# A two-layer diffusion step on one Trainium2 core: low parts of a weight corner, copies of products, convolution taps, one tile's scaling and one pair of transposes issued in another sequence

## The chip, the cores and the metric

The kernel runs on one core of one Trainium2 chip. The metric is the time of one execution on the device in microseconds (us). Of before there are three timed runs and one profiled run.

## What is computed

One inference step of a trunk of two layers, on 512 latent tokens and 128 prompt tokens of width 1024. Layer 0 mixes tokens by neighbourhood attention on a 2-D grid, layer 1 by grouped-query attention. After each mixer stands a gated ConvFFN of width 2816, each sub-layer between two RMS norms, with shift, scale and gate from a conditioning vector (adaLN). Cut to the part in which most of the change lies:

```python
def conv_ffn(h, w_up, conv_w, conv_b, w_down):
    u = h @ w_up
    up = jnp.pad(u, ((0, 0), (1, 1), (0, 0)))
    u = up[:, :-2] * conv_w[0] + up[:, 1:-1] * conv_w[1] + up[:, 2:] * conv_w[2] + conv_b
    a, gt = jnp.split(u, 2, axis=-1)
    return (jax.nn.silu(a) * gt) @ w_down
```

All is float32; the outputs are the two token streams and the new keys and values of both layers.

## The kernel before, in words

**Two parts for each operand.** Each float32 weight or activation is cast on ScalarE to a high part (`wh`, `vh`, `ah`, `B`, `hF`'s parts) and the rest goes into a low part (`wl`, `vl`, `al`), a `tensor_sub` on VectorE or GpSimd. A product is three passes: high x high, low x high, high x low. `wsplit` (L170) does this for a weight on its way in, `split` (L1291) inside the ffn.

**The up-projection.** In `ffn` the hidden width is cut into 22 pieces of 128, p = 0 to 21, each with a value half (i = 0) and a gate half (i = 1). The 640 tokens are two halves of `TH` = 320. For p = 0 and 1 (`PLAIN` = 2) `plain0` and `plain1` multiply the weight's halves plainly. From p = 2 on, the 2 x 2 blocks of weight and activation are multiplied with seven products in the place of eight (a Winograd form): `product(m, p)` is product m, twelve matmuls of 128x320. `of_m` says which weight block each takes: product 6 and 3 the sum `(0, p)`, product 7 and 5 the sum `(1, p)`, product 1 and 2 the value block `w`, product 4 the corner `a`. The weights' sums are formed by `block_sums` (four `wr` instructions on VectorE, L1314 to L1317, in place in the raw weights, so that the fourth can only follow the corner's `al`, which reads them); `sum_parts` casts them to `wh` (ScalarE) and `wl` (GpSimd from p = 3 on); `value` and `corner` make `vh`/`vl` and `ah`/`al`.

**The order of products.** For each p the loop at L1488 runs m = 6, 5, 1 of p+1, 7, 2 of p+1, 3, 4. `evict` takes each out of PSUM: `copied` (ScalarE copies `c1`, `u2`, `v5`), sums into the convolution's input `C` on VectorE (L1400, L1409, L1413), and a copy for product 4 (L1417). After product 3, `conv_value` runs the width-3 convolution of the value half: `t` on ScalarE (L1378), two taps on VectorE (L1381, listed in `taken`), then SiLU, `sl`. After product 4, `conv_gate` does the same for the gate half and multiplies (`act`, L1392, `marks[4]`); `store` sends it to DRAM. In layer 0 a group of 24 adaLN matmuls (`ada`) stands between some of the products.

**The down-projection.** `load_dn` (L1248) brings a weight and an activation piece `ain` back, casts it (`ahi`) and forms its low part `alo` on VectorE (L1261; the list `lows`). The accumulators are `acc`. At the end of a layer `Finish` makes the residual, the norm and the next sub-layer's input: `shifted` (L416) scales a token tile in two halves, `turns` transposes it.

**What sets the order.** TensorE's instructions are chained one behind the other (`pe`, L111), so that their order is the order of the program text. For the other engines a scheduler sets the order, from data and buffers; `behind(a, b)` (L125) adds that `a` comes after `b`. Each engine then runs its list strictly in that order, each instruction waiting for its data and for the release of the buffer that it writes.

**The attention's end.** In layer 0 the query and key projections run as a stream of small steps (`stream`, L1115) between the heads. Each head pair ends with `tail`, which transposes the prompt's new keys (`tk`, for the output). Behind the stream, `early` begins the output projection, `m0.part0(t, p)`, tile `y`.

Of the kernel before, what the change touches and what calls it, by code (L numbers as in the profile page):

```python
# [105 lines left out]
def hybrid_step(ctx: ExitStack, tc: tile.TileContext, A, O):  # L106
# [57 lines left out]
    def x_in(t):  # L164
        return A["x_sample"][0, t * P : (t + 1) * P, :] if t < 4 else A["x_prompt"][0]

    queue = []


    def wsplit(src, a, b, low=None, own=None, pin=False, after=None, high=None, low_after=None):  # L170
        q = own or wp
        raw = wp.tile([P, a, b], F32, tag="wr", name="wr")
        i = nc.sync.dma_start(raw, src)
        if queue:
            behind(i, queue.pop())
        hi = q.tile([P, a, b], F32R, tag="wh", name="wh")
        i = nc.scalar.copy(hi, raw)  # L177
        lo = q.tile([P, a, b], F32R, tag="wl", name="wl")
        j = (low or nc.vector).tensor_sub(lo, raw, f32(hi))  # L179
        if high:  # L180
            behind(i, high[0])
        if after:
            behind(i, after[0])
            behind(j, after[1])
        if low_after and not low:
            behind(j, low_after)
        if pin:
            tc.keep_in_program_order(i)
            tc.keep_in_program_order(j)
        return hi, lo  # L190
# [148 lines left out]
    class Finish:  # L339
# [75 lines left out]

        def shifted(self, t):  # L416
            xm, r = self.xm[t]
            return [
                nc.vector.scalar_tensor_tensor(
                    xm[:, c], xm[:, c], r, self.sh[:, c], op0=ALU.mult, op1=ALU.add  # L420
                )
                for c in HALF
            ][0]

        def last(self, copied, added, low):

# [420 lines left out]
    with l_na:  # L847
# [253 lines left out]
            nc.vector.tensor_sub(lo, of0[p], f32(hi))  # L1101


        items, marks = [], {}

        def put_qk(p):
            it, tail = na_qk_items(p)
# [10 lines left out]
        def stream():  # L1118
            items[0][0]()
            tail = None  # L1120
            for n, (load, parts) in enumerate(items):
                for i, part in enumerate(parts):
                    part()
                    if n + 1 == len(items) and i in OW:
                        m0.weights(0, OW[i], nc.gpsimd)
                    if i == 1 and n + 1 < len(items):
                        items[n + 1][0]()
                    if i == 4 and tail:
                        tail()
                        tail = None  # L1130
                    yield
                tail = marks.get(n + 1, tail)
            if tail:
                tail()

        work = stream()
        l_ada = ExitStack()
# [14 lines left out]
        for h in range(H):  # L1152
            nxt = Head(h + 1) if h + 1 < H else None
            g = h // 4
            pr = h % 4 == 1
            order = (ORDER if h < 13 else ORDER2)[h % 2] if h else ORDER0
            for i, step in enumerate(order):
                if step == "f":
                    if i < len(order) - 1 or h % 4 or not h:
                        fill()  # L1160
                elif step == "a":
                    next(ada0, None)
                elif step[0] == "s" and nxt:
                    nxt.scores(int(step[1]))
                elif step[0] == "t":
                    head.turns(int(step[1]))
                elif step == "v":
                    values((before, head))
                if pr and step == "p0":
                    sides = []  # L1170
                    for hh in range(4 * g, 4 * g + 4):
                        qs, kh, kl = qk_of[hh // 2]
                        b = hh % 2
                        sides.append((qs[b][:, QW - P :], kh[b][:, T:], kl[b][:, T:]))
                    pp = prompt_scores(ap, sides)
                if pr and step == "p1":
                    pth = prompt_turn(ap, pp, "pk", NPK)
                if pr and step == "p2":
                    po = bk.get("po")
                    for j in range(2):  # L1180
                        for b in range(2):
                            mm(po[64 * b : 64 * b + 64, j * P : j * P + P], vts_of[g][:, 4, 2 * j + b, :],
                               pth[:, 2 * j + b, :], start=True, stop=True)
                    for j in range(2):
                        nc.scalar.copy(of0[2 * g + j][:, NS:T], po[:, j * P : j * P + P])
                    bk.put(po)
            before = head
            head = nxt
            if h == 11:
                def early(ps, *rows_):  # L1190
                    for ts in rows_:
                        for p in ps:
                            for t in ts:
                                m0.part0(t, p)
                                yield

                work = chain(work, early(range(OEARLY), range(2)))
                drain(ada0)
                l_ada.close()
                epool = l_na.enter_context(pool("o0e", 1))  # L1200
                osp0.extend([epool.tile([P, T], F32R, name=f"o{i}{p}") for i in "hl"] for p in range(OEARLY))
                for p in range(OEARLY):
                    o_split(p)
            if h == 12:
                drain(work)
                r_h0.close()
                hpool = r_na.enter_context(pool("o0h", 1, "right"))
                osp0.extend([hpool.tile([P, T], F32R, name=f"o{i}{p}") for i in "hl"] for p in range(OEARLY, KC))
                for p in range(OEARLY, 4):
                    o_split(p)  # L1210
                m0.weights(0, 3)
                for p in range(4, 6):
                    o_split(p)

                work = chain(early(range(OEARLY, 6), range(2)), early(range(6), range(2, NT)))
            if h == 13:
                o_split(6)
# [21 lines left out]
    def ffn(l, hT, hT_close, xold, xnew, nxt, todo, late, late_close, side, back, first, fin0, after=None):  # L1239
# [33 lines left out]
        with ExitStack() as s2:  # L1273
# [15 lines left out]
                return [own.tile([P, n, P], F32R, tag=x, name=x) for x in tags]  # L1289

            def split(src, hl, low):  # L1291
                nc.scalar.copy(hl[0], src)  # L1292
                return low.tensor_sub(hl[1], src, f32(hl[0]))  # L1293

            def plain(p, i, low):
# [9 lines left out]

            def corner(p):
                ws["a", p] = pair_of(sw2, ("ah", "al"), 4)
                split(raws[p, 1][:, 4:8, :], ws["a", p], nc.vector)

            def block_sums(p):  # L1310

# [10 lines left out]
                done.add((p, i))  # L1322
                fetch()

            banks, cs, ts, small, outs, taken, marks, held = {}, {}, {}, {}, deque(), [], {}, []

            def block_product(u, w, h, b, first, last=True, lows=False):

# [67 lines left out]
            def evict(m, p, u):  # L1396
# [5 lines left out]
                elif m == 6:  # L1402
                    copied("u2", p, u)
                elif m == 5:
                    copied("v5", p, u)
                elif m == 7:
                    v = small.pop(("v5", p))
                    for c, dst in pieces(p, 1):
                        marks[7] = nc.vector.tensor_add(dst, u[:, c], v[:, c])  # L1409
                elif m == 3:  # L1410
                    v = small.pop(("u2", p))
                    for c, dst in pieces(p, 0):
                        marks[3] = nc.vector.tensor_add(dst, u[:, c], v[:, c])  # L1413
                    bk.put(banks.pop(("z", p)))
                    conv_value(p)
                else:
                    nc.scalar.copy(block(p, 1, 0), u)  # L1417
                    bk.put(banks.pop(("x", p)))
                    conv_gate(p)
# [52 lines left out]
            for n, c in enumerate(chunks):  # L1472
                plain1(*c)
                if n == 1:
                    corner(PLAIN)
                    block_sums(PLAIN)
                    sum_parts(0, PLAIN, nc.vector)
                    sum_parts(1, PLAIN, nc.vector)
                    drain(more)
            value(PLAIN + 1, nc.gpsimd)  # L1480
            corner(PLAIN + 1)
            bk.drop(4)
            psy.close()
            ct = s2.enter_context(pool("ct", space=PSUM))
# [12 lines left out]
            for p in range(PLAIN, FC):  # L1497
                nx = p + 1 if p + 1 < FC else None
                for m, q in ((6, p), (5, p), (1, nx), (7, p), (2, nx), (3, p), (4, p)):
# [7 lines left out]
                            lds.append(load_dn(len(lds), *HB[0], after=taken[-3]))  # L1507
                    elif m == 7:
                        store()
                        if nx:  # L1510
                            sum_parts(0, nx, nc.gpsimd)
                        else:
                            behind(lows[0], marks[7])
                            if ada and not nxt:
# [6 lines left out]
                    elif m == 3:  # L1521
                        if not nx:
                            lds.append(load_dn(len(lds), *HB[0], low=False))
                            behind(lows[1], marks[3])
                            behind(taken[-2], lows[1])
                        elif nx + 1 < FC:
                            corner(nx + 1)
                    if ada:
# [17 lines left out]
        for grp, (c0, c1) in (((0, 1, 2), HB[0]), ((3, 4), HB[1])):  # L1546
# [8 lines left out]
            for k in range(FC - tail):  # L1555
                if len(lds) <= k:
                    lds.append(load_dn(k, c0, c1, after=taken[-3] if k == 2 and c0 == 0 else None))
                for t in grp:
                    if t != 2 or k >= DLEAD:
                        go(t, k, *lds[k])  # L1560
# [10 lines left out]
            for t in grp:  # L1571
# [7 lines left out]
                for i in range(tail):  # L1579
# [4 lines left out]
                        lds.append(load_dn(len(lds), *HB[1]))  # L1584
                    if t == 4 and after:
                        after(i)
                late.append(fin.end(t, acc[t][0], acc[t][1], fin.stat(acc[t][0])))
        fin.close()
        s.close()
# [502 lines left out]
```

## Time and profile before

| what | value |
|---|---|
| median of three timed runs | 1532.52 us (1531.22 to 1532.67) |
| profiled run, its own time | 1531.28 us |
| span of the profiled run | 1529.5 us |
| mean granted TensorE clock | 0.998 |
| TensorE (PE) busy | 1506.5 us, 98% of the span |
| VectorE (DVE) busy | 1029.7 us, 67% |
| ScalarE (ACT) busy | 853.6 us, 56% |
| GpSimd (POOL) busy | 701.1 us, 46% |

The span runs from the first to the last instruction; the run's own time holds 1.8 us more around it. PE is the matmul engine, PEld its weight load. In a timeline a row gives the start in us, how long it lasted, engine, line, operation, what was written and read with its shape, and in brackets how long the engine had been idle before and what released it. In the list of waits a row gives the engine and tile that waited, what for, the us in total, how often, and the longest.

### The profile page before, as it was taken

Reading aid. Unit: us, or ns where it says so; the run is one execution under the profiler, and the core shown is the slowest. Engines: PE = TensorE matmul, PEld = TensorE weight load, DVE = VectorE, ACT = ScalarE, POOL = GpSimd, SP = SyncE. Lnnn points to the kernel's source line nnn. Section 1 sums busy time; section 2 is a strip of 40 time slices with the busy share of each in tenths; the row PEclk is TensorE's granted clock in tenths of the full one; section 3 lists DMA queues with packets and bytes.
Section 4 is the critical chain, followed back from the end, with each engine's and each line's share of the span. In section 5 each row is a group of like instructions: output and inputs, shape, how many; then the busy total and the mean of one; then the engine's idle time right before and its main releaser. Section 6 shows DMA issues by size and latency. Waiting matters only on the chain.

```text
span 1529.5 us, 26196 instructions
## 1 busy us (share of the span) xinstructions
PE 1506.5 (98%) x9710; PEld 1338.6 (88%) x9710; DVE 1029.7 (67%) x1733; ACT 853.6 (56%) x1636; POOL 701.1 (46%) x572
## 2 busy tenths in 40 slices
PE   7999999999999999999999999999999999999998
PEld 6989989789999999988887878778899999998886
DVE  5544443659877667865748878773988888886454
ACT  5665564646655555654545447763666665564343
POOL 1655554332355455534444454442235665553433
PEclk9999999999999999999999999999999999999999
DMA  9755444263575655388575421015433334458663
GB/s 351 186 137 150 121 132 115 64 206 111 183 231 182 226 189 160 123 283 272 189 221 161 124 75 38 2 41 189 157 114 118 112 120 150 133 162 280 216 224 131
DMA packets 196667, 243.99 MB, mean 160 GB/s; under 512 B 11485, under 2 KB 153021, under 8 KB 196541
## 3 DMA queue, kind: packets, MB, share of 16 engines
q1 hardware_dynamic: 186924, 235.85, 47.7%
q10 hardware_dynamic: 9616, 6.48, 2.4%
q8 instruction: 76, 1.25, 0.3%
q14 instruction: 51, 0.41, 0.1%
HBM read 214.38 MB, written 26.34 MB: 157 GB/s over the span
## 4 chain that ended last, share of the span: by engine, by line
PE 66%; DVE 7%; issue 1%; ACT 1%; POOL 1%; DMA 0%; DVEq 0%; POOLq 0%; ACTq 0%
PE acc L118 19%; PE ux L118 17%; PE uz L118 9%; PE gp L118 5%; PE uy L118 4%; PE y L118 3%; PE po L118 2%; PE s L118 2%; PE tp L121 2%; PE ada L118 2%; DVE B L248 1%; DVE wl L179 1%; DVE nmg L1813 1%; DVE t L1381 0%; DVE pk L1832 0%
## 5 line engine op out<-in xcount | busy, mean ns | idle before, releaser
L1293 POOL TENSOR_TENSOR wl<-wr,wh 128x1024 fp32r<-128x1024 f32 x76 | 181.5, 2411 | 222.1 <-ACT wh L1292 211.4
L179 POOL TENSOR_TENSOR wl<-wr,wh 128x1024 fp32r<-128x1024 f32 x70 | 172.1, 2461 | 233.6 <-ACT wh L177 219.0
L118 PE MATMUL ux<-B,wh 128*128 128x320 f32 x832 | 198.7, 311 | 0.9 <-ACT u L1348 0.8
L1381 DVE SCALAR_TENSOR_TENSOR t<-C,cw,t 128x642 f32<-128x642 f32 x176 | 156.0, 886 | 48.6 <-ACT t L1378 48.0
L118 PE MATMUL acc<-wh,ahi 128*128 128x512 f32 x440 | 172.1, 391 | 0.3 <-DVE act L1392 0.3
L118 PE MATMUL acc<-wh,alo 128*128 128x512 f32 x440 | 172.2, 391 | 0.0
L118 PE MATMUL acc<-wl,ahi 128*128 128x512 f32 x440 | 172.0, 391 | 0.0
L177 ACT CAST wh<-wr 128x1024 fp32r<-128x1024 f32 x138 | 143.3, 1048 | 41.6 <-DMA wr<-in_ffn_w_down 31.9
L118 PE MATMUL uz<-B,wh 128*128 128x320 f32 x640 | 154.6, 310 | 0.0
L118 PEld LDWEIGHTS ux<-B,wh 128*128 128x128 f32 x832 | 142.8, 188 | 4.1 <-ACT u L1348 1.3
L1261 DVE TENSOR_TENSOR alo<-ain,ahi 128x384 fp32r<-128x384 f32 (+1 forms) x88 | 80.2, 928 | 85.3 <-ACT ahi L1259 84.3
L118 PE MATMUL ux<-B,wl 128*128 128x320 f32 x416 | 128.8, 310 | 0.0
L118 PE MATMUL qk<-hT,wh 128*128 128x384 f32 (+1 forms) x512 | 122.4, 315 | 0.0
L118 PEld LDWEIGHTS uz<-B,wh 128*128 128x128 f32 x640 | 110.4, 188 | 2.9 <-issue 1.2
L1292 ACT CAST wh<-wr 128x1024 fp32r<-128x1024 f32 x84 | 85.0, 1048 | 48.2 <-DVE wr L1317 47.8
L1293 POOL TENSOR_TENSOR vl<-wr,vh 128x1024 fp32r<-128x1024 f32 x38 | 99.1, 2609 | 21.7 <-ACT vh L1292 21.6
L179 DVE TENSOR_TENSOR wl<-wr,wh 128x1024 fp32r<-128x1024 f32 x68 | 89.1, 1324 | 20.3 <-ACT wh L177 19.7
L1378 ACT ACTIVATE t<-C,cw 128x642 f32<-128x642 f32 x88 | 78.5, 892 | 42.1 <-DVE C L1413 33.5
L118 PE MATMUL uz<-B,wl 128*128 128x320 f32 x320 | 99.0, 309 | 0.0
L118 PEld LDWEIGHTS acc<-wh,ahi 128*128 128x128 f32 x440 | 82.6, 188 | 18.3 <-issue 0.7
L118 PEld LDWEIGHTS acc<-wl,ahi 128*128 128x128 f32 x440 | 82.6, 188 | 17.9
L118 PEld LDWEIGHTS acc<-wh,alo 128*128 128x128 f32 x440 | 82.6, 188 | 17.6
(263 smaller groups left out, 3858.8 us busy)
## 6 DMA issues: line engine op xcount, KB each, us to landing
wr<-in_ffn_w_up SPq DMA_DIRECT2D x88, 512.0 KB
wr<-in_ffn_w_down SPq DMA_DIRECT2D x88, 512.0 KB
wr<-in_ada_w SPq DMA_DIRECT2D x72, 512.0 KB
act<-act SPq DMA_DIRECT2D x44, 321.0 KB
wr<-in_na_w_qkv SPq DMA_DIRECT2D x24, 512.0 KB
mod<-modrow SPq DMA_DIRECT2D x20, 512.0 KB
ain<-act SPq DMA_DIRECT2D x44, 192.0 KB
wf<-in_ada_w SPq DMA_DIRECT2D x16, 512.0 KB
```

What stands on the lines that cost most here:

```text
L118: pe(nc.tensor.matmul(*a, **k))
L121: pe(nc.tensor.transpose(*a, **k))
L177: i = nc.scalar.copy(hi, raw)
L179: j = (low or nc.vector).tensor_sub(lo, raw, f32(hi))
L248: return nc.vector.tensor_sub(lo, src, f32(hi))
L1261: i = nc.vector.tensor_sub(lo[:, 0 : c1 - c0], ain[:, 0 : c1 - c0], f32(hi[:, 0 : c1 - c0]))
L1292: nc.scalar.copy(hl[0], src)
L1293: return low.tensor_sub(hl[1], src, f32(hl[0]))
L1378: nc.scalar.activation(t, taps(0), AF.Identity, bias=cw[:, 3, n : n + 1], scale=cw[:, 1, n : n + 1])
L1381: nc.vector.scalar_tensor_tensor(t, taps(d), cw[:, w, n : n + 1], t, op0=ALU.mult, op1=ALU.add))
L1813: self.red[i] = nc.vector.tensor_reduce(nm, sv, axis=AX.XY, op=ALU.min)
```

## The change

The arithmetic, the tiles and the number of matmuls stay as they are. Five places get another sequence.

1. The last head pair's `tail` (the transposes `tk`) is not issued at the end of the stream but by `early`, behind the first `m0.part0` of tile 1 (list `ends`).
2. At the ffn's start the low part `al` of the corner of p = 2 goes behind the fourth `plain0` sum (`summed[1]`).
3. The low part `al` of the corner of p = 3 goes behind the last sum of product 7 of p = 2 (`marks[7]`); the cast `wh` of the sum `(0, 3)` goes behind the copy `v5` of p = 2 (`marks[5]`).
4. Around the first loads of the down-projection the ties of `alo` change: the second goes behind the last tap, the fourth behind `act`, and a tap is no longer behind the second.
5. At the end of layer 0 the two halves of the scaling of token tile 3 go behind the low part `wl` of the weight loaded last.

The diff, cut to its core:

```diff
 def wsplit(...):
         j = (low or nc.vector).tensor_sub(lo, raw, f32(hi))
+        lowered[:] = [j]
...
 def stream():
-            if tail:
-                tail()
+            ends.append(tail)
...
                             for t in ts:
                                 m0.part0(t, p)
+                                if ends and t:
+                                    ends.pop()()
                                 yield
...
             def split(src, hl, low):
-                nc.scalar.copy(hl[0], src)
+                i = nc.scalar.copy(hl[0], src)
+                high[:] = [i]
                 return low.tensor_sub(hl[1], src, f32(hl[0]))
...
                 elif m == 5:
-                    copied("v5", p, u)
+                    marks[5] = copied("v5", p, u)
...
                 if n == 1:
-                    corner(PLAIN)
+                    behind(corner(PLAIN), summed[1])
                     block_sums(PLAIN)
...
             value(PLAIN + 1, nc.gpsimd)
-            corner(PLAIN + 1)
+            low = corner(PLAIN + 1)
...
                     elif m == 7:
                         store()
+                        if p == PLAIN:
+                            behind(low, marks[7])
                         if nx:
                             sum_parts(0, nx, nc.gpsimd)
+                            if p == PLAIN:
+                                behind(high[0], marks[5])
...
                             lds.append(load_dn(len(lds), *HB[0], low=False))
-                            behind(lows[1], marks[3])
-                            behind(taken[-2], lows[1])
+                            behind(lows[1], taken[-1])
...
                     lds.append(load_dn(k, c0, c1, after=taken[-3] if k == 2 and c0 == 0 else None))
+                    if k == 3 and c0 == 0:
+                        behind(lows[k], marks[4])
...
                     if t == 4 and after:
                         after(i)
+                        if i == tail - 1:
+                            for j in fin.moved:
+                                behind(j, lowered[0])
```

`corner` returns its low part, and `shifted` keeps its two instructions in `self.moved`. TensorE's order differs in the transposes `tk` alone. On the other engines the scheduler's order changes at more places than the ties name. The instructions below are listed by line, operation, tile with buffer number and shape; line numbers after the change are a few higher.

ScalarE in layer 0, around products 6 of p = 2 to 4 of p = 2, before. `wh_4928` and `wh_4948` are the casts of the two sums of p = 3, `ah_4997` that of the corner of p = 4, `vh_4954` that of its value block:

```order
L1292 CAST wh_4928<-wr_4435 128x1024
L1348 COPY u2_4868<-ux_4430 128x320
L1292 CAST wh_4948<-wr_4503 128x1024
...
L1292 CAST vh_4954<-wr_4739 128x1024
L1378 ACTIVATE t_4842<-C1_4582,cw0_82 128x2x321
L1387 ACTIVATE sl_4846<-t_4842 128x642
L1378 ACTIVATE t_4848<-C1_4582,cw0_82 128x2x321
L1292 CAST ah_4997<-wr_4745 128x512
```

ScalarE at the same place, after:

```order
L1295 CAST vh_4954<-wr_4739 128x1024
L1383 ACTIVATE t_4842<-C1_4582,cw0_82 128x2x321
L1392 ACTIVATE sl_4846<-t_4842 128x642
L1295 CAST ah_4997<-wr_4745 128x512
L1383 ACTIVATE t_4848<-C1_4582,cw0_82 128x2x321
L1295 CAST wh_4928<-wr_4435 128x1024
L1295 CAST wh_4948<-wr_4503 128x1024
```

The two casts `wh` have moved from around the copy `u2` of p = 2 to behind `ah_4997` and the next `t`. In layer 1 they stand likewise behind `ah`, the copy `C`, `sl` and `t`. On GpSimd the low part `vl` of p = 4 now stands ahead of the two `wl` of p = 3.

VectorE in layer 0, from the corner of p = 3 on, before (`al_4809` is its low part, the four `wr` are the sums, `t` the conv taps):

```order
L1293 TENSOR_TENSOR al_4809<-wr_4503,ah_4808 128x512
L1314 TENSOR_TENSOR wr_4503<-wr_4503 128x512
L1315 TENSOR_TENSOR wr_4503<-wr_4435,wr_4503 128x512
L1316 TENSOR_TENSOR wr_4435<-wr_4503,wr_4435 128x512
L1317 TENSOR_TENSOR wr_4435<-wr_4435 128x512
L1381 SCALAR_TENSOR_TENSOR t_4830<-C0_4465,cw0_82,t_4830 128x2x321 x2
L1381 SCALAR_TENSOR_TENSOR t_4836<-C0_4465,cw0_82,t_4836 128x2x321
L1409 TENSOR_TENSOR C2_4660<-ux_4430,v5_4893 128x192
L1381 SCALAR_TENSOR_TENSOR t_4836<-C0_4465,cw0_82,t_4836 128x2x321
```

VectorE, the stretch with the same `al_4809` and `wr`, after:

```order
L1386 SCALAR_TENSOR_TENSOR t_4836<-C0_4465,cw0_82,t_4836 128x2x321
L1414 TENSOR_TENSOR C2_4660<-ux_4430,v5_4893 128x128
L1297 TENSOR_TENSOR al_4809<-wr_4503,ah_4808 128x512
L1397 TENSOR_TENSOR act_4840<-t_4836,sl_4834 128x642
L1318 TENSOR_TENSOR wr_4503<-wr_4503 128x512
L1405 TENSOR_TENSOR C0_4465<-uy_4934,c1_4912 128x320
L1386 SCALAR_TENSOR_TENSOR t_4842<-C1_4582,cw0_82,t_4842 128x2x321
L1319 TENSOR_TENSOR wr_4503<-wr_4435,wr_4503 128x512
L1386 SCALAR_TENSOR_TENSOR t_4842<-C1_4582,cw0_82,t_4842 128x2x321
L1320 TENSOR_TENSOR wr_4435<-wr_4503,wr_4435 128x512
L1418 TENSOR_TENSOR C2_4660<-uz_4880,u2_4868 128x192
L1321 TENSOR_TENSOR wr_4435<-wr_4435 128x512
```

Low part and sums of p = 3 have moved from ahead of the conv taps to among them, behind the sum into `C2` of product 7.

ScalarE at the start of the Winograd products in layer 0, before (`wh_4735` and `wh_4741` are the casts of p = 2's sums, `B40` a high part of a sum of activation blocks, `C` copies of plain products):

```order
L1292 CAST wh_4735<-wr_4426 128x1024
L1443 COPY C0_4465<-ux_4470 128x192
L1443 COPY C0_4465<-ux_4470 128x128
L1292 CAST wh_4741<-wr_4428 128x1024
L247 CAST B40_4669<-hF_3985 128x1280
```

After:

```order
L1448 COPY C0_4465<-ux_4470 128x192
L1448 COPY C0_4465<-ux_4470 128x128
L248 CAST B40_4669<-hF_3985 128x1280
L1295 CAST wh_4735<-wr_4426 128x1024
L1295 CAST wh_4741<-wr_4428 128x1024
```

The cast `B40` has moved ahead of both `wh`, and the copies `C0` too.

More of the change, by code (lines that the diff above doesn't have):

```diff
@@ L165, in x_in @@
         return A["x_sample"][0, t * P : (t + 1) * P, :] if t < 4 else A["x_prompt"][0]
-    queue = []
+    queue, lowered = [], []
     def wsplit(src, a, b, low=None, own=None, pin=False, after=None, high=None, low_after=None):
@@ L417, in shifted @@
             xm, r = self.xm[t]
-            return [
+            self.moved = [
                 nc.vector.scalar_tensor_tensor(
@@ L422, in shifted @@
                 for c in HALF
-            ][0]
+            ]
+            return self.moved[0]
         def last(self, copied, added, low):
@@ L1101, in o_split @@
             nc.vector.tensor_sub(lo, of0[p], f32(hi))
-        items, marks = [], {}
+        items, marks, ends = [], {}, []
         def put_qk(p):
@@ L1307, in corner @@
                 ws["a", p] = pair_of(sw2, ("ah", "al"), 4)
-                split(raws[p, 1][:, 4:8, :], ws["a", p], nc.vector)
+                return split(raws[p, 1][:, 4:8, :], ws["a", p], nc.vector)
             def block_sums(p):
@@ L1323, in sum_parts @@
                 fetch()
-            banks, cs, ts, small, outs, taken, marks, held = {}, {}, {}, {}, deque(), [], {}, []
+            banks, cs, ts, small, outs, taken, marks = {}, {}, {}, {}, deque(), [], {}
+            held, high = [], []
             def block_product(u, w, h, b, first, last=True, lows=False):
```

## The prediction, made before the change was run

> **What bounds the kernel now.** I read the page first, for its busy times and its chain, then TensorE's list of waits, then the timeline of each engine around every place that the change touches. The first lines of the page, and the first line of the chain that ended last:
>
> ```profile
> span 1529.5 us, 26196 instructions
> ## 1 busy us (share of the span) xinstructions
> PE 1506.5 (98%) x9710; PEld 1338.6 (88%) x9710; DVE 1029.7 (67%) x1733; ACT 853.6 (56%) x1636; POOL 701.1 (46%) x572
> ...
> PE 66%; DVE 7%; issue 1%; ACT 1%; POOL 1%; DMA 0%; DVEq 0%; POOLq 0%; ACTq 0%
> ```
>
> TensorE works through 98% of the span and carries two thirds of the chain. Its order of matmuls is fixed, so the time moves only by what TensorE waits for. These are the rows of its waits that the change can reach (engine and tile, what it waited for: us in total, times, longest):
>
> ```profile
> PE ux L118 <- DVE C L1409: 1.6, 2, 0.9
> ...
> PE tk L121 <- ACT kp L974: 0.8, 1, 0.8
> PE ux L118 <- ACT u L1348: 0.8, 2, 0.4
> PE uy L118 <- DVE C L1433: 0.6, 2, 0.3
> ...
> PE gp L118 <- DVE wl L179: 0.4, 1, 0.4
> ...
> PE acc L118 <- DVE act L1392: 0.3, 1, 0.3
> ```
>
> Together they are 4.5 us: no more can be won here. What can be lost has no such lid, and depends on how much slack the moved work has where it stands.
>
> **Part 1, the transposes of the last keys.** TensorE's 0.8 us at `tk` goes, since six matmuls of the output projection run ahead of it. But soon after them TensorE needs the low part `kl`, on VectorE:
>
> ```profile
> 281.58 1.13 DVE L929 TENSOR_TENSOR kl<-qk,kh 64x384 fp32r<-64x384 f32 x2
> ```
>
> VectorE's work up to there does not hang on `tk`. TensorE comes earlier and waits longer for the same instruction: 0, with bounds of -0.8 and 0.
>
> **Part 2, the start of the ffn.** The low part `al` of the corner for p=2 stood ahead of the sum `C` for which TensorE waited twice (0.6 in all); that goes. The rest of the row of work is reshuffled: on ScalarE the cast `B40` now stands ahead of the two casts `wh` of p=2's sums.
>
> ```profile
> 385.59 1.27 ACT L247 CAST B<-hF 128x1280 fp32r<-128x1280 f32 x1
> ```
>
> So these casts, and the low parts behind them, come up to 1.27 later, which can take back the 0.6. The casts of p=3's sums also leave the place where the copy `u` waited (0.8 in all, two times); that goes too. But all this lies ahead of a new wait of TensorE, below, whose end does not hang on how early TensorE arrives: the wait swallows it. I put part 2 at 0.
>
> **Part 3, the corner and the sums of p=3, is the term that decides.** Per p TensorE runs products 6, 5, 1 (of the next p), 7, 2 (of the next p), 3, 4, each of 12 matmuls. Product 6 of p=3 follows product 4 of p=2 at once, and its second matmul reads `wl(0,3)`. In layer 0, before:
>
> ```profile
> 402.20 0.31 PE L118 MATMUL ux<-B,wh 128*128 128x320 f32 x1
> 402.35 0.31 PE L118 MATMUL ux<-B,wl 128*128 128x320 f32 x1
> ...
> 404.12 0.31 PE L118 MATMUL uz<-B,wl 128*128 128x320 f32 x1
> ```
>
> `wl` is needed at 402.35, and product 5 needs the other one, `wl(1,3)`, 1.77 later at 404.12. On GpSimd both were ready at 393.12 + 4.74 = 397.86, 2.37 each:
>
> ```profile
> 393.12 4.74 POOL L1293 TENSOR_TENSOR wl<-wr,wh 128x1024 fp32r<-128x1024 f32 x2 [4.11 <-ACT wh L1292]
> ```
>
> Now ScalarE, before. The first row is one of the casts `wh` of p=3, the last the cast `ah` for p=4's corner:
>
> ```profile
> 391.99 1.05 ACT L1292 CAST wh<-wr 128x1024 fp32r<-128x1024 f32 x1 [2.93 <-DVE wr L1317]
> ...
> 403.16 0.71 ACT L1387 ACTIVATE sl<-t 128x642 f32<-128x642 f32 x1 [1.88 <-DVE t L1381]
> 403.90 0.89 ACT L1378 ACTIVATE t<-C,cw 128x642 f32<-128x642 f32 x1
> 404.73 0.60 ACT L1292 CAST ah<-wr 128x512 fp32r<-128x512 f32 x1
> ```
>
> After the change the two casts stand behind `sl`, `ah` and `t` (the piece of ScalarE's order above). Their tie, to the copy `v5`, would ask for far less: the sums that they read became late on VectorE, and the rest of ScalarE's queue went ahead. So `wl(0,3)` cannot be there before `sl` + `ah` + `t` + `wh` + `wl`.
>
> When does `sl` start? In the profile it waits for the two conv taps ahead of it on VectorE:
>
> ```profile
> 401.31 1.82 DVE L1381 SCALAR_TENSOR_TENSOR t<-C,cw,t 128x642 f32<-128x642 f32 x2 [0.56 <-ACT t L1378]
> ```
>
> Ahead of the second tap now stand the low part `al` and two of the sums `wr`. Their price, in a place where `al` ran beside GpSimd's `vl`, VectorE first, then GpSimd:
>
> ```profile
> 417.34 2.75 DVE L1293 TENSOR_TENSOR al<-wr,ah 128x512 fp32r<-128x512 f32 x1
> 420.12 0.69 DVE L1314 TENSOR_TENSOR wr<-wr 128x512 f32<-128x512 f32 x1
> ```
> ```profile
> 417.11 2.43 POOL L1293 TENSOR_TENSOR vl<-wr,vh 128x1024 fp32r<-128x1024 f32 x1
> ```
>
> Two instructions of one shape: 0.69 alone, 2.75 when GpSimd had begun just before. So `sl` gets 3 x 0.69 = 2.1 us more ahead of it, or 4.1 with `al` held like that. On the other side ScalarE no longer idles 2.93 for the sums ahead of its table load, and a cast of 1.05 leaves: 3.98 less. `sl` then starts between 403.16 - 3.98 + 2.1 = 401.3 and 403.16 - 3.98 + 4.1 = 403.3. I take 402.2: `al` meets the tail of `vl`, which moves up too, not the whole of it.
>
> The Trainium skill ("SBUF — State Buffer", Who interferes with whom) says that a VectorE instruction with two inputs in SBUF and a GpSimd instruction that reads SBUF exclude each other, the later one blocked until the first has ended. The rows at 417 agree; by the rule taken whole `sl` would be at the upper end, 403.3, and the sum 1.1 per layer larger.
>
> From 402.2: 0.71 + 0.60 + 0.89 + 1.05 + 2.37 = 5.62, so `wl(0,3)` is there at 407.8, and TensorE is 5.45 behind. Bounds: `ah` reuses the buffer that product 4 of p=2 reads, so it can't start before that product ends, about 402.0 (402.20 less some 0.2 that part 2 wins ahead of it); 402.0 + 4.91 = 406.9. From 403.3: 408.9. Product 5 then needs `wl(1,3)`, 2.37 later against the 1.77 that TensorE takes: another 0.6, or 1.3 if a sum of 0.69 on VectorE gets between the two on the way; I take 0.9. What comes behind has slack: `vl` of p=4 now runs ahead of both. One wait goes, the longer of the two for `C` (0.9, in p=4 of layer 0): there TensorE is late and VectorE is not. Layer 0: 5.45 + 0.9 - 0.9 = +5.4, between 4.55 + 0.6 - 0.9 = 4.2 and 6.55 + 1.3 = 7.9.
>
> Layer 1 has the same products, without the adaLN matmuls between 3 and 4. TensorE, then ScalarE, before:
>
> ```profile
> 1134.26 0.41 PE L118 MATMUL ux<-B,ah 128*128 128x320 f32 x1 [0.69 <-DVE C L1409]
> ...
> 1136.28 0.31 PE L118 MATMUL ux<-B,wl 128*128 128x320 f32 x1
> ```
> ```profile
> 1136.33 0.62 ACT L1292 CAST ah<-wr 128x512 fp32r<-128x512 f32 x1 [0.46 <-PE ux L118]
> 1136.86 0.42 ACT L1417 COPY C<-ux 128x320 f32<-128x320 f32 x1
> 1137.76 0.71 ACT L1387 ACTIVATE sl<-t 128x642 f32<-128x642 f32 x1 [0.48 <-DVE t L1381]
> 1138.49 0.89 ACT L1378 ACTIVATE t<-C,cw 128x642 f32<-128x642 f32 x1
> ```
>
> The first row of ScalarE shows `ah` waiting for TensorE's product 4. Here the order after is `ah`, `C`, `sl`, `t`, `wh`, `wh`. `sl` moves as in layer 0, from 1137.76 by -0.96 to 1136.8; 0.71 + 0.89 + 1.05 + 2.37 = 5.02 more gives 1141.8, against 1136.28: +5.5, and 0.9 for product 5: +6.4. The wait of 0.69 is in it already. Bounds: `ah` at 1136.33 - 0.69 = 1135.6, or 0.4 sooner with what part 2 wins, 1135.2, with everything close behind, 1135.2 + 0.62 + 0.42 + 5.02 = 1141.2 with small overlaps, so 4.9 + 0.6 = 5.5; 1.1 later, 6.6 + 1.3 = 7.9.
>
> **Part 4, the down-projection's first loads.** In layer 0 the last two conv taps and `act` no longer stand behind a low part `alo`. The wait of `acc` for `act`, 0.3, goes; that `alo` is late instead would cost the same: -0.3, bounds -0.3 and +0.3. Layer 1 shows no such wait: 0.
>
> **Part 5, the scaling of tile 3.** The four low parts `wl` of the next projection now come first, and `gp` waits for one of them, 0.4: -0.4. The scaling then ends later, and its transposes stand right behind; bounds -0.4 and 0.
>
> **The sum.** 5.4 + 6.4 - 0.3 - 0.4 = +11.1, against the profiled run, 1531.28 (span 1529.5): 1542.4. That run lies 1.24 under the median of 1532.52, so 1543.6 on the median. All low bounds: 4.2 + 5.5 - 0.3 - 0.4 - 0.8 = +8.2, 1540.7. All high ones: 7.9 + 7.9 + 0.3 = +16.1, 1548.6.
>
> **The rivals.** First, the clock. TensorE has no wait of 5 us in these stages today. One place shows what a thin stretch can bring:
>
> ```profile
> 16.00:20.00 4.00, 3.29 (x37) 2.24 (x29) 2.62 (x10) 2.57 (x6) 0.00 (x0) 1.00 1.09 385
> 20.00:24.00 4.00, 3.92 (x27) 3.22 (x31) 3.86 (x8) 2.80 (x7) 0.00 (x0) 0.62 1.11 346
> ```
>
> Right after four us in which TensorE was busy for 3.29 (second column), the granted clock (third number from the end) is 0.62 for four: 1.52 us lost. If each stall is followed by the same, TensorE loses up to 1.5 each, of which up to 0.9 lies in the wait for `wl(1,3)` anyhow: +0.6 to +1.5 a layer, middle 2.1 for both, 1545.7. For it: both stalls would be far longer than any wait in the rows above. Against it: what the threshold is, no row tells. The Trainium skill ("TensorE: Matmul & The Clock Gate", What's actually happening) says that an idle window of about 3.4 us halves the clock until a busy window of that length has passed; by it both stalls would be hit, with up to 1.7 us each. The trace agrees in kind, with its 1.52.
>
> Second, on the other side: the sums are in time. If the casts reached ScalarE's head by 402.35 - 2.37 - 1.05 = 398.9, TensorE would not wait, and only removed waits would count: 1.6 + 0.8 + 0.6 + 0.4 + 0.3 = 3.7, so 1528.8. For it: before the change 402.35 - 397.86 leaves 4.5 us of slack even for the second `wl`. Against it: ScalarE would have to pass `ah` 3 us before product 4 of p=2 has ended.
>
> Third, layer 0 hides it, by the adaLN matmuls between its products 3 and 4, and layer 1 alone pays: 6.4 - 0.9 - 0.3 - 0.4 = +4.8, 1537.3. Against it: these matmuls stood there before as well, and 402.35 counts them in.
>
> Fourth, what is won and lost cancels, 1532.5: it would need a stall of under 4 us in all. That the change does nothing is out: the orders differ.
>
> **How the numbers follow.** The forecast, both layers wait at full clock, 0.55; with the clock, 0.28; layer 1 alone, 0.06; no change, 0.04; in time, 0.07. About 0.2% (3.1 us) is what a measurement can tell from no change: slower 0.55 + 0.28 + 0.06 = 0.89, same 0.04, faster 0.07. A range from 1539.5 leaves out the last three cases, 0.17; up to 1549.5 it takes in the high bounds and most of the clock's.
>
> **What would show it.** In the profile after, TensorE's waits should have `ux` and `uz` at the head, for `wl` of GpSimd, four times: some 5.5 and 0.9 in layer 0 near 402 to 411, some 6 and 0.9 in layer 1 near 1135 to 1144. ScalarE should show `wh` behind `ah`. The rows for `C` L1409, `u`, `uy` and `gp` should be gone or smaller, that for `sp` larger by what `tk` lost. The granted clock there tells the first rival. If TensorE runs from product 4 into product 6 without a gap, the prediction is wrong.

## The result, and the profile after

| | before | after |
|---|---|---|
| median | 1531.93 us (6 runs, 1530.73 to 1532.67) | 1544.15 us (6 runs, 1544.04 to 1545.46) |
| ratio to before | | 1.0082, 95% interval 1.0069 to 1.0095 |
| profiled run, span | 1531.28, 1529.5 us | 1544.20, 1542.1 us |
| mean granted clock | 0.998 | 0.993 |

The change costs 12.2 us between the medians; 11.1 were forecast, 1543.6 us. The page of the profile after, its first lines:

```profile
span 1542.1 us, 26200 instructions
## 1 busy us (share of the span) xinstructions
PE 1507.9 (98%) x9710; PEld 1341.7 (87%) x9710; DVE 1028.1 (67%) x1733; ACT 855.0 (55%) x1636; POOL 701.3 (45%) x572
```

TensorE has the same 9710 matmuls and is busy for 1.4 us more; the rest of the 12.6 us of span is waiting. Its list of waits after (us in total, times, longest):

```profile
PE ux L118 <- ACT wh L1295: 7.4, 2, 4.3
PE ux L118 <- POOL wl L1297: 4.6, 2, 2.4
PE ux L118 <- DVE wl L1297: 1.6, 2, 0.8
PE sp L118 <- DVE kl L931: 1.4, 1, 1.4
```

The first two rows are new and belong together: at product 6 of p=3, in each layer, TensorE waits for `wh`, runs one matmul, and waits for `wl`. The rows for `C` L1409, `u`, `uy`, `gp` and `acc` are gone. The third row is a wait for the low parts of p=2, whose casts now stand behind `B40`. The fourth is the 0.8 of `tk`, met again at `sp`, where 0.4 stood before.

Since TensorE's order is the same in both kernels, each matmul can be laid beside itself. Start of the same matmul in the two traces, us:

| place | before | after | difference |
|---|---|---|---|
| `qk`, near the start | 100.07 | 99.26 | -0.8 |
| `sp`, behind `tk` | 282.34 | 281.54 | -0.8 |
| product 5 of p=3 done, layer 0 (`ux<-B,vh`) | 405.73 | 412.73 | +7.0 |
| its first `wl` ahead of that, product 6 | 402.35 | 407.35 | +5.0 |
| product 4 of p=4, layer 0 | 427.77 | 433.69 | +5.9 |
| down-projection, layer 0 | 700.09 | 705.42 | +5.3 |
| next projection, `gp` | 814.19 | 818.78 | +4.6 |
| product 4 of p=2, layer 1 | 1134.26 | 1138.02 | +3.8 |
| first `wl` of product 6 of p=3, layer 1 | 1136.28 | 1147.03 | +10.8 |
| product 5 of p=3 done, layer 1 | 1139.66 | 1152.86 | +13.2 |
| last matmul | 1522.65 | 1535.37 | +12.7 |

The -0.8 at 100 us is no gain of the change, which touches nothing there: the two runs differ in their first 40 us, where one had a spell of half clock and the other not (see the end).

Layer 0, ScalarE after, then TensorE after:

```profile
401.46 0.71 ACT L1392 ACTIVATE sl<-t 128x642 f32<-128x642 f32 x1 [3.33 <-DVE t L1386]
402.07 0.61 ACT L1295 CAST ah<-wr 128x512 fp32r<-128x512 f32 x1
402.58 0.89 ACT L1383 ACTIVATE t<-C,cw 128x642 f32<-128x642 f32 x1
403.40 1.98 ACT L1295 CAST wh<-wr 128x1024 fp32r<-128x1024 f32 x2
```
```profile
404.49 0.42 PE L118 MATMUL ux<-B,wh 128*128 128x320 f32 x1 [3.11 <-ACT wh L1295]
407.35 0.64 PE L118 MATMUL ux<-B,wl 128*128 128x320 f32 x1 [2.44 <-POOL wl L1297]
407.78 0.73 PE L118 MATMUL ux<-B,wh 128*128 128x320 f32 x2
```

`sl` was put at 402.2 and began at 401.46; `wl(0,3)` was put at 407.8 and let TensorE go at 407.35. This run was 0.8 ahead from its start, though: without that, the two would stand at 402.3 and 408.2. On VectorE the sum that stood beside `vl` was stretched to 1.66, and `al` was not; VectorE, then GpSimd:

```profile
395.77 0.68 DVE L1297 TENSOR_TENSOR al<-wr,ah 128x512 fp32r<-128x512 f32 x1
...
398.97 1.66 DVE L1319 TENSOR_TENSOR wr<-wr 128x512 f32<-128x512 f32 x1
```
```profile
397.43 2.65 POOL L1297 TENSOR_TENSOR vl<-wr,vh 128x1024 fp32r<-128x1024 f32 x1 [10.68 <-ACT vh L1295]
404.51 5.57 POOL L1297 TENSOR_TENSOR wl<-wr,wh 128x1024 fp32r<-128x1024 f32 x2 [4.43 <-ACT wh L1295]
```

Layer 1, ScalarE after, then TensorE after:

```profile
1141.62 0.71 ACT L1392 ACTIVATE sl<-t 128x642 f32<-128x642 f32 x1 [0.69 <-DVE t L1386]
...
1143.19 1.97 ACT L1295 CAST wh<-wr 128x1024 fp32r<-128x1024 f32 x2
```
```profile
1144.27 0.64 PE L118 MATMUL ux<-B,wh 128*128 128x320 f32 x1 [4.33 <-ACT wh L1295]
1147.03 0.64 PE L118 MATMUL ux<-B,wl 128*128 128x320 f32 x1 [2.12 <-POOL wl L1297]
```

The matmuls behind these waits are slow, 0.73 for two where 0.46 is usual. The table of stretches of three us shows why (the column behind the engines is the granted clock):

```profile
400.00:403.00 3.00, 1.38 (x10) 1.11 (x8) 3.00 (x6) 1.53 (x3) 0.08 (x1) 1.00 1.03 393
403.00:406.00 3.00, 0.42 (x1) 0.19 (x1) 3.00 (x6) 2.70 (x4) 1.49 (x1) 0.79 0.24 97
406.00:409.00 3.00, 1.65 (x6) 1.65 (x7) 3.00 (x3) 0.00 (x0) 3.00 (x2) 0.50 0.12 30
409.00:412.00 3.00, 3.00 (x15) 3.00 (x13) 2.37 (x3) 1.31 (x3) 1.07 (x1) 0.57 0.63 183
412.00:415.00 3.00, 3.00 (x23) 3.00 (x22) 1.73 (x2) 2.95 (x5) 2.05 (x1) 1.00 0.79 250
...
1141.00:1144.00 3.00, 0.00 (x0) 0.00 (x0) 2.96 (x6) 2.35 (x3) 0.00 (x0) 0.67 0.00 0
1144.00:1147.00 3.00, 0.64 (x1) 0.29 (x1) 3.00 (x4) 1.16 (x2) 2.71 (x2) 0.50 0.02 5
1147.00:1150.00 3.00, 2.98 (x11) 2.98 (x12) 3.00 (x3) 0.89 (x1) 2.76 (x1) 0.50 0.55 164
1150.00:1153.00 3.00, 3.00 (x15) 3.00 (x14) 2.90 (x5) 0.43 (x1) 0.00 (x0) 0.62 0.53 144
```

The clock fell to half in both stalls and stayed there for a while after them: the first rival of the prediction happened.

### The profile page after: what moved, and what is told of

It reads as the page before. It is cut to its first block, busy times and chain, and to the rows that moved or that the text cites. A ratio compares the mean times of both kernels' runs of the same rounds, so it can differ in the third digit from the quotient of the medians.

```text
span 1542.1 us, 26200 instructions
## 1 busy us (share of the span) xinstructions
PE 1507.9 (98%) x9710; PEld 1341.7 (87%) x9710; DVE 1028.1 (67%) x1733; ACT 855.0 (55%) x1636; POOL 701.3 (45%) x572
## 4 chain that ended last, share of the span: by engine, by line
PE 65%; DVE 5%; issue 2%; DMA 1%; POOL 1%; ACT 1%; ACTq 0%; DVEq 0%; POOLq 0%
PE acc L118 20%; PE ux L118 17%; PE uz L118 9%; PE uy L118 4%; PE gp L118 4%; PE y L118 2%; PE po L118 2%; PE s L118 2%; PE tp L121 2%; PE ada L118 2%; DVE B L249 1%; DMA wr<-in_ffn_w_up 1%; DMA gn<-in_gqa_k_norm 1%; DVE nmg L1826 1%; DVE wl L179 0%
## 5 line engine op out<-in xcount | busy, mean ns | idle before, releaser
L1264 DVE TENSOR_TENSOR alo<-ain,ahi 128x384 fp32r<-128x384 f32 (+1 forms) x88 | 74.0, 855 | 86.9 <-ACT ahi L1262 86.6
L1262 ACT CAST ahi<-ain 128x384 fp32r<-128x384 f32 (+1 forms) x88 | 39.6, 460 | 105.6 <-PE acc L118 93.2
```

The costliest lines, as they stand in the source:

```text
L1262: pin(nc.scalar.copy(hi[:, 0 : c1 - c0], ain[:, 0 : c1 - c0]))
L1264: i = nc.vector.tensor_sub(lo[:, 0 : c1 - c0], ain[:, 0 : c1 - c0], f32(hi[:, 0 : c1 - c0]))
```

## The experiments

Each experiment's ratio is to runs of the kernel before on the same chip (medians 1531.16 and 1531.28 us there). One kernel's runs spread by 1 to 4 us, and at 100 us the traces already lie up to 3.2 us apart, so a difference under a microsecond is read from where in the traces it stands.

**Without part 3.** Both ties of p=3 are taken out:

```diff
                         store()
-                        if p == PLAIN:
-                            behind(low, marks[7])
...
                             sum_parts(0, nx, nc.gpsimd)
-                            if p == PLAIN:
-                                behind(high[0], marks[5])
```

> The changed kernel without part 3: neither the low part al nor the cast wh of p=3 is tied; parts 1, 2, 4 and 5 stay. Theory (part 3 alone makes the two long stalls): what is left is, by the shifts between the two traces, tk +0.2, uy -0.5 and -0.4, the new wait for wl of p=2 +0.85 and +0.8, the down-projection -0.5, the scaling of tile 3 -0.9, together about -0.3 us: 1531.6 us, ratio to before 0.9998; no wait of TensorE over 1 us near 402 and 1136, clock 1.00 there. Rival (part 2's reshuffle of ScalarE makes the casts late, part 3 only adds): still over 1538 us.

Measured: 1530.56 us, ratio 0.9994, interval 0.9985 to 1.0004. No long wait is left; the waits for `u` and `C` are back:

```profile
PE ux L118 <- ACT u L1353: 1.7, 2, 0.9
PE ux L118 <- DVE C L1414: 1.6, 2, 0.9
```

So part 3 makes the loss, and the four other parts together move nothing that can be measured. One thing was not as expected: the wait for `wl` of p=2 did not show; the wait for `u` grew by 0.9 in all in its place.

**Part 3 alone**, put into the kernel before:

```diff
             value(PLAIN + 1, nc.gpsimd)
-            corner(PLAIN + 1)
+            low = corner(PLAIN + 1)
...
+                        if p == PLAIN:
+                            behind(low, marks[7])
...
+                            if p == PLAIN:
+                                behind(high[0], marks[5])
```

> The kernel before with part 3 alone. Theory (part 3 alone makes the stalls; the rest is worth some -0.6): both stalls at product 6 of p=3 with the half clock behind them, +12 to +14 us: 1543.5 to 1545.5 us. Rival (part 3 needs part 2's reshuffle to do harm): under 1538 us.

Measured: 1545.73 us, ratio 1.0096, interval 1.0081 to 1.0112, clock 0.992. Against before, TensorE's matmuls move by 3.3 and 2.7 at product 6 of p=3 in layer 0 and by 4.5 and 2.6 in layer 1, which are the steps of the changed kernel. It needs no help of part 2. The 14.4 us are a little over the expected 12 to 14; counted from 100 us in the traces they are 14.3, against 13.5 with all five parts.

**Which of the two ties?** First without the tie of `al`, then without that of the cast:

```diff
-                        if p == PLAIN:
-                            behind(low, marks[7])
```

> The changed kernel with the cast wh of the sum (0,3) still tied to the copy v5, but al no longer tied to product 7. Theory (the tie of al holds back the four sums wr, and with them the casts; the cast's own tie is harmless): both wl of p=3 are ready near 400, before TensorE needs them at 402; the copy u2 is no longer held by a cast, so two waits of 0.45 go as well: about -1.2 us or a little more, 1529.5 to 1531.0 us, no long stall. Rival (the cast's tie costs by itself): a stall of 2 us or more at product 6 of p=3 in each layer, over 1535 us.

Measured: 1528.46 us, ratio 0.9981, interval 0.9973 to 0.9990: faster than both kernels, and by more than expected. GpSimd in this kernel, layer 0:

```profile
398.31 4.77 POOL L1297 TENSOR_TENSOR wl<-wr,wh 128x1024 fp32r<-128x1024 f32 x2 [5.90 <-ACT wh L1295]
```

Both `wl` are ready at 403.1, later than expected but in time: TensorE runs from product 4 into product 6 without a gap and reads the second one at 404.38. By the shifts TensorE stands 3.8 us ahead of before at product 4 of p=2 in layer 1, and 2.5 of it are given back over the next three p, in small waits of TensorE for `wl` and `C`:

```profile
PE uz L118 <- POOL wl L1297: 0.5, 2, 0.3
PE ux L118 <- POOL wl L1297: 0.5, 1, 0.5
```

```diff
                             sum_parts(0, nx, nc.gpsimd)
-                            if p == PLAIN:
-                                behind(high[0], marks[5])
```

> The changed kernel with al still tied to product 7, but the cast wh no longer tied to v5. Theory: ScalarE's order is the same as in the changed kernel, since the sums wr come late whatever the cast's tie says: 1544.2 us, within 1 us, both stalls as in the changed kernel. Rival (the cast's tie matters): under 1538 us.

Measured: 1544.83 us, ratio 1.0086, interval 1.0072 to 1.0100. Same loss, to the tenth at each step. The tie of `al` alone decides. Of the four sums `wr` it is the first that overwrites the corner, which `al` reads, and the others build on it; so all four must follow `al`, and not the fourth alone, as the description of the kernel before could be read.

**Is it the place behind `ah`, or the sums?**

```diff
                         sum_parts(1, nx, nc.gpsimd)
+                        cast = high[0]
...
                             corner(nx + 1)
+                            if p == PLAIN:
+                                behind(high[0], cast)
```

> The changed kernel with the corner's cast ah of p=4 tied behind both casts wh of p=3's sums, so that on ScalarE the casts no longer stand behind ah, which waits for TensorE's product 4 (sl, C, t still stand ahead of them). Theory A, as the prediction put it (the casts are held by their place behind ah): wl(0,3) comes about 0.6 sooner in layer 0 and up to 1.6 sooner in layer 1: 1542.0 to 1543.0 us. Theory B (the last of the four sums wr ends on VectorE only 0.1 to 0.5 us before the casts start, and the taps that sl and t need end as late, so the place behind ah adds nothing): 1544.2 us, within 0.6, and wh starts within 0.3 us of where it does in the changed kernel.

Measured: 1543.79 us, ratio 1.0082, interval 1.0068 to 1.0095. ScalarE's casts, with `ah` now behind them:

```profile
403.43 1.04 ACT L1295 CAST wh<-wr 128x1024 fp32r<-128x1024 f32 x1
```

403.40 in the changed kernel, in a run that is 0.2 behind here: theory B. In layer 1 they start at 1142.91 against 1143.19, in a run that is 0.3 ahead there. Taking `ah` away moves the casts by 0.2 at most. `sl`, `t` and the copy `C` (which in layer 0 has moved into the place of `ah`) keep them there, and in the changed kernel the last sum of VectorE ends only 0.5 us (layer 0) and 0.1 us (layer 1) before the casts start. What this run did win lies behind the casts. The first `wl` lasts 2.36 in both layers, against 2.79 and 2.68 in the changed kernel, where VectorE ran a sum or `al` beside its start; so TensorE goes on 0.6 and 0.3 sooner (the 0.6 is theory A's figure, but not by its cause). And in layer 1 the half clock lasts 3.4 us less than in the changed kernel:

```profile
1147.00:1150.00 3.00, 3.00 (x15) 3.00 (x14) 3.00 (x2) 0.38 (x1) 2.15 (x1) 0.62 0.66 188
1150.00:1153.00 3.00, 3.00 (x23) 3.00 (x22) 2.96 (x5) 1.51 (x4) 0.00 (x0) 1.00 0.87 256
```

**Is it GpSimd's `vl` that stretches the sum?** `split` hands its low part back, and that of `vl` is tied:

```diff
-                            value(nx + 1, nc.gpsimd)
+                            v = value(nx + 1, nc.gpsimd)
+                            if p == PLAIN:
+                                behind(v, lowest[0])
```

`lowest` is the low part of the last `sum_parts`.

> The changed kernel with the low part vl of p=4 tied behind the low parts wl of p=3 on GpSimd, which is its order before the change. Theory (vl, running at 397.4 to 400.1, holds up the sum wr of VectorE, which lasts 1.66 there and not 0.69, and everything behind it): that sum lasts 0.7, sl starts about 1.0 sooner, wl(0,3) is ready 0.6 to 1.0 sooner in each layer, and vl still comes in time for product 1 of p=4: 1542.3 to 1543.3 us. Rival (the stretch has another cause, or ah takes over as what comes last): 1544.2 us; or vl is now late for product 1: 1545 us or more.

Measured: 1544.83 us, ratio 1.0091, interval 1.0077 to 1.0105. The sum is no longer stretched:

```profile
402.15 0.68 DVE L1319 TENSOR_TENSOR wr<-wr 128x512 f32<-128x512 f32 x1
```

The cause of the stretch is shown. Counted from TensorE's product 4 the first `wl` is ready 0.75 and 0.8 sooner, as the theory had it, but the time did not follow. Laid beside the changed kernel, TensorE gains 0.6 us over the stall in layer 0 (3.53 behind ahead of it, 2.91 after product 5) and 0.5 in layer 1 (3.15, 2.68); but this run came 3.2 us later out of its first 100 us, and the medians do not resolve the gain. In layer 0 it was now `ah`, waiting for product 4, that came last, as the rival had it:

```profile
404.94 0.62 ACT L1295 CAST ah<-wr 128x512 fp32r<-128x512 f32 x1 [0.56 <-PE ux L118]
```

**The clock.** TensorE gets 24 matmuls more in the stall:

```diff
+                    if m == 6 and p == PLAIN + 1:
+                        x = spare["z", p] = bk.get("uz")
+                        for i in range(24):
+                            mm(x[:, 0:TH], ws["w", p + 1][0][:, i % 4, :], hT.B["11"][0][:, i % 4, :], start=i == 0,
+                               stop=i == 23, skip_group_check=True)
                     evict(m, q, product(m, q))
```

> The changed kernel with 24 more matmuls of 128x320 ahead of product 6 of p=3 in each layer, on weights and activations that lie ready, into the PSUM bank that product 5 starts afresh right after, so that no result changes. They last 3.5 us and start when that bank is free, near 403 in layer 0 and 1143 in layer 1, so TensorE should be done with them about when the awaited wl is ready. Theory (the clock drops because TensorE stands still for over 3 us, and the half clock adds to the stall): in layer 0 the clock stays at 1.00, product 6 runs at 0.147 us per matmul, and TensorE waits again for wl(1,3); layer 0 ends 1.0 us sooner than in the changed kernel; in layer 1, where it still stands still for 3.3 us first, between 0 and 1.4 sooner: 1541.8 to 1543.2 us. Rival (the slow matmuls there come from something else, such as the reading of a weight just written): spacing stays at 0.29 us and the time is 1544.2 us or more.

Measured: 1543.45 us, ratio 1.0077, interval 1.0064 to 1.0091. A bank was free at once, so they began when the stall did. Layer 1, TensorE:

```profile
1140.14 3.68 PE L118 MATMUL uz<-B,vh 128*128 128x320 f32 x24
1144.64 0.41 PE L118 MATMUL ux<-B,wh 128*128 128x320 f32 x1 [0.82 <-ACT wh L1295]
1147.39 0.41 PE L118 MATMUL ux<-B,wl 128*128 128x320 f32 x1 [2.34 <-POOL wl L1297]
1147.65 0.46 PE L118 MATMUL ux<-B,wh 128*128 128x320 f32 x2
...
1150.19 0.41 PE L118 MATMUL uz<-B,wl 128*128 128x320 f32 x1 [0.77 <-POOL wl L1297]
```

and the clock there and, as the second row, in layer 0:

```profile
1147.00:1150.00 3.00, 2.03 (x12) 1.76 (x12) 3.00 (x3) 0.69 (x2) 3.00 (x2) 1.00 0.47 134
...
409.00:412.00 3.00, 3.00 (x13) 2.78 (x13) 2.97 (x3) 1.59 (x3) 1.32 (x1) 0.54 0.66 180
```

In layer 1 the clock stays at 1.00, two matmuls take 0.46, and the wait for `wl(1,3)` appears, 0.77. Against the changed kernel TensorE goes from 0.36 us behind (product 4 of p=2) to 0.95 ahead (after product 5): 1.3 us is what the half clock cost there, net of that wait. That the slow matmuls came from reading a weight just written is out, for here they read the same weight at full pace. In layer 0 a spell of half clock came all the same, later, behind the 2.3 us in which TensorE still waits, and only 0.3 us is won. The expectation held in layer 1 and failed in layer 0.

**A better place for the casts?** Without the tie of `al`, the cast tied to `u2`, and `tk` back at its old place:

```diff
                 elif m == 6:
-                    copied("u2", p, u)
+                    marks[6] = copied("u2", p, u)
...
-                                behind(high[0], marks[5])
+                                behind(high[0], marks[6])
...
-            ends.append(tail)
+            if tail:
+                tail()
```

> The changed kernel without the tie of al (as in the run without it), the cast wh of (0,3) tied to the copy u2 instead of v5, and the transposes tk back at the end of the stream. Theory: TensorE no longer waits for u2, and the casts run 3 us earlier than behind v5, so that the low parts of p=3 to 5 in layer 1 come sooner and less of the gain is given back there; tk at its old place is worth 0.2: 0.997 to 0.998 of before, some 1527 to 1528 us. Rival (what is given back in layer 1 is set by VectorE's load and not by where the casts stand, and the table load and sl now stand behind two casts, so the waits for C come back): 0.998 to 1.000, as without the tie of al or slower.

Measured: 1529.78 us, ratio 0.9990, interval 0.9982 to 0.9999. My theory falls, the rival holds: 2.8 us ahead of before in layer 1 at product 4 of p=2, of which 2.6 are gone by product 4 of p=5, 1.6 of them in a wait for `C`. Behind `v5` looks the better place: counted from 100 us, the trace with the cast there ends 2.5 us ahead of before and this one 1.4. The intervals of the two ratios overlap, so the times alone do not tell them apart.

## Why the prediction came out right, point by point

- **Part 3, the term that decides: right in mechanism, in place, and nearly in size, with some luck.** In the table the first `wl` of product 6 goes from 0.8 early (at 100 us) to 5.0 late in layer 0, by 5.8, put at 5.45. In layer 1 the difference grows from 4.8 at 1100 us to 10.75, by 5.9, put at 5.5. `sl` stood where it was put in both layers (402.3 for 402.2; 1141.62 for 1136.8 + 4.8 = 1141.6), but the price ahead of it was paid by another instruction: `al` was to be held beside `vl` and was not, a sum was. That the two prices are alike is luck. What is missing, 0.35 and 0.4, is for the most part the first `wl`, which lasted 2.79 and 2.68 and not 2.37. In both layers TensorE arrived at the wait early and this was swallowed, as said.
- **The reason that it gave for the casts' late place was only half of it.** It held that `ah`, waiting for product 4, sets the lower bound. Without `ah` ahead of them the casts start at the same time, within 0.2. It is the sums on VectorE, and the taps for `sl` and `t` beside them, that are late.
- **Product 5, 0.9 per layer: too small.** From that first `wl` to the end of product 5 the difference grew by 2.0 in layer 0 and 2.4 in layer 1. The waits for `wl(1,3)` that were forecast do not show: the half clock stretched product 6 over them. In layer 1 the run with the filled stall has the wait of 0.77 in place of it, and gains 1.3.
- **The clock was given as a rival, 0.28; it happened.** The forecast "at full clock" was the wrong case of the two, by a net 1.3 us in layer 1, where the experiment could show it; for layer 0 no run shows it whole. An estimate for layer 0: both `wl` are ready at 404.51 + 5.57 = 410.08; at full clock TensorE would have needed the second at 407.35 + 1.77 = 409.12 and waited 1.0 of the 2.0 that it lost, so the clock cost the other 1.0. By the rows above the clock lost (0.21 + 0.50 + 0.43) x 3 = 3.4 us in layer 0 and (0.33 + 0.50 + 0.50 + 0.38) x 3 = 5.1 in layer 1; most of it lay in the waits themselves. The Trainium skill ("TensorE: Matmul & The Clock Gate", What's actually happening) has an idle window of about 3.4 us before and a busy one of that length after. The half clock lasted 6.8 and 10.2 us here, two and three times 3.4, which agrees. The 3.4 us before were not empty, though: in layer 1, from 1138.63 to the fall at 1142.04, TensorE was busy for 1.31.
- **Part 1: 0 was put down, at best -0.8.** The wait moved to `sp`, 1.4 for 0.4; the difference is -0.81 before and -0.80 behind. Right in this trace. In three of the other traces with the moved transposes the half clock followed that wait and cost some 0.4 to 0.5 us (see the end); this was not thought of.
- **Part 2:** the wait of `uy` went and was given back: -0.5, then +0.85 and +0.8 for `wl` of p=2, then -0.45 for `u`. Swallowed in any case, as forecast. Without part 3 that wait for `wl` does not come, although `B40` stands ahead of both casts there too. The traces differ on VectorE: in the changed kernel GpSimd's `vl` (373.10, 3.44 us) lies beside `hF` (L262), which lasts 3.33; without part 3 `vl` begins at 377.10 and the same `hF` lasts 1.48. No run tests this alone.
- **Parts 4 and 5:** -0.3 and -0.4 were put down; at these places the difference fell by 0.5 and by 0.8 (at two places of `gp`, 0.2 and 0.7, of which the list had shown one). Each is the wait with what follows it until TensorE is at its pace again.
- **The sum:** 5.4 and 6.4 per layer against 6.7 (from -0.8 to +5.9) and 8.0 (from +4.8 at 1100 us to +12.8 at 1177): low by 2.9, of which the clock explains 1.3 in layer 1 and, by the estimate, 1.0 in layer 0; most of the rest is the longer `wl`. Parts 4 and 5 take back 0.6. Between the traces, from -0.8 at 100 us to +12.7 at the end, that is 13.5 for the 11.1 forecast. Of the medians' 12.2 the forecast missed only 1.1, and part of that closeness is luck: the trace after was 0.8 ahead from its start, and the trace before is a run 0.65 under its median. It is luck too that 1543.6 lies 0.55 under the measured 1544.15, for its base of 1532.52, a median of three, was 0.6 above that of six.

## What to carry to other kernels

A tie that looks like one instruction moves all that overwrites what it reads: here one low part of 0.7 us took four sums, two casts and two GpSimd subtractions with it, through three engines. Before such a tie is added, walk from the tied instruction to the next use on the busiest engine and count each queue's own length; here it used up the slack of 4.5 us and 5.8 us of TensorE besides, in layer 0 alone. And of a stall on TensorE count more than its length: the half clock that followed the stalls here had a price of its own, 1.3 us in layer 1, and in some traces it followed waits of 2.3 and 1.4 us as well.

## What the runs showed of the hardware that was not expected

GpSimd was shut out here for as long as VectorE had a run of instructions with two inputs in SBUF, not for one instruction only. In the run without the tie of `al`, GpSimd's `vl`, then the VectorE instructions in the same stretch:

```profile
378.06 13.85 POOL L1297 TENSOR_TENSOR vl<-wr,vh 128x1024 fp32r<-128x1024 f32 x1 [12.12 <-ACT vh L1295]
```
```profile
378.05 0.68 DVE L1318 TENSOR_TENSOR wr<-wr 128x512 f32<-128x512 f32 x1
378.66 2.89 DVE L249 TENSOR_TENSOR B<-hF,B 128x1280 fp32r<-128x1280 f32 x2
...
388.94 0.68 DVE L1319 TENSOR_TENSOR wr<-wr 128x512 f32<-128x512 f32 x1
391.94 0.69 DVE L1320 TENSOR_TENSOR wr<-wr 128x512 f32<-128x512 f32 x1 [2.32 <-POOL vl L1297]
```

The same `vl` takes 3.45 before. Here VectorE leaves no gap from 378.05 to 389.6, `vl` lasts 13.85, and then VectorE in turn waits 2.32 for it to end. These 2.3 us are about what a `vl` takes undisturbed (2.38 to 2.43). Without part 3 it lasted 13.85 too, and with the cast behind `u2` 13.86.

The first 40 us differ from trace to trace, though the change touches nothing there. In the profile before, the granted clock is 0.62 at 20 to 24 us; after, it is 1.00 there, though TensorE was no busier in the four us ahead:

```profile
16.00:20.00 4.00, 3.12 (x27) 2.25 (x28) 2.17 (x9) 2.30 (x4) 0.00 (x0) 1.00 1.09 386
20.00:24.00 4.00, 4.00 (x49) 2.85 (x49) 3.86 (x7) 2.54 (x7) 0.21 (x1) 1.00 1.12 357
```

The traces without part 3 and with part 3 alone show the fall at 20 us as well, two others show one at 35 us.

At the wait for `sp`, too, the half clock came in some traces (without part 3, without the cast's tie, with `ah` behind the casts) and not in the changed kernel, with TensorE about as busy just ahead. Without part 3, then the changed kernel:

```profile
280.00:283.00 3.00, 1.57 (x11) 1.31 (x10) 2.91 (x6) 2.96 (x9) 2.26 (x3) 1.00 0.17 63
283.00:286.00 3.00, 3.00 (x12) 2.56 (x12) 3.00 (x7) 3.00 (x6) 1.66 (x2) 0.56 0.58 188
```
```profile
280.00:283.00 3.00, 1.62 (x10) 1.55 (x11) 2.91 (x7) 2.98 (x9) 2.26 (x3) 1.00 0.23 59
283.00:286.00 3.00, 2.91 (x16) 2.08 (x15) 3.00 (x6) 3.00 (x8) 1.02 (x1) 1.00 0.39 140
```

The three traces with `tk` at its old place (before, part 3 alone, the cast behind `u2`) show none there. How much idleness within a stretch makes the clock fall stays open.
